# Three edits to an encoder layer: a second tile for v's parts with h written in pairs, w_out queued behind the first pages of y, and eight slices for the last h2

## The chip, the cores and the metric

The kernel runs on one core of one Trainium2 chip. The metric is device time in microseconds (us) for one execution of the whole layer, the median of the runs; the time before is 2748.61 us. A core has a matrix engine (TensorE, "PE" in the profile, with its weight loads as "PEld"), a vector engine (VectorE, "DVE"), an engine for activation functions (ScalarE, "ACT"), a general one (GpSimd, "POOL") and a sequencer that here only issues transfers (SyncE, "SP"). Each works through its own queue in order. ScalarE's queue also issues transfers (`A.dma_start`).

## The reference

One layer of an encoder with two kinds of attention side by side, 2048 tokens of width 1024, all in float32:

```
h  = RMSNorm(x)
z  = h @ W_in  -> [q_A | k_A | v_A | q_B | k_B | v_B | gate_A | gate_B]
yA = windowed GQA over |t-s| <= 128 with ALiBi and per-head sink logit
yB = 2-D neighbourhood attention on the (ROWS, GRID_W) token grid with a relative position bias
x  = x + ( sigmoid(gate_A) * (yA @ Wp_A) + sigmoid(gate_B) * (yB @ Wp_B) ) @ W_out
x  = x + relu(RMSNorm(x) @ W_up)^2 @ W_down
final RMSNorm
```

W_in is 1024 x 4352, Wp_A and Wp_B are 512 x 1024, W_out is 1024 x 1024, W_up is 1024 x 4096 and W_down 4096 x 1024.

## The kernel before

**Precision and products.** Every float32 operand of a large product is split into a high part (`hi`, a cast on ScalarE) and a low part (`lo`, a subtraction on VectorE or GpSimd), and each product is three matmuls (`mm3`, lines 193 to 195, or `mm3s`, lines 239 to 241): high by high, high by low, low by high. Tokens are worked on in four blocks of 512 (`b`, 0 to 3). Data on the chip lies transposed, features on the 128 partitions. The dense stage, the up projection and the down projection use a scheme of seven block products in place of eight (products 1 to 7, in the order 1, 2, 5, 6, 7, 4, 3 in the dense stage and 1, 5, 6, 2, 7, 4, 3 in the up projection). A group of columns that is put through the seven products is called a quad; in a quad each product has one or two column halves (`a`) of 12 matmuls.

**Order.** The code is not the order of execution. A planner, which works on its own estimate of times when the kernel is built, orders each engine's queue, with earlier code first when several things are ready, and adds the waits. A ring or pool with n buffers lets the (n+1)-th tile of that name be written only when the first has been read for the last time, by transfers too; memory of a closed pool goes to later pools, whose tiles wait for the old tiles on the same bytes. `tc.issue_after(i)` puts what is issued in its block on the engine of `i` behind `i` in that engine's queue; it does not wait for `i` to finish.

**Stages.**
- The dense stage computes z. Blocks 0 and 1 of x are normalised and transposed into pages of h that stay on the chip, and quads 0 to 8 of W_in's columns run over those two blocks: k and v of A, q of A, q of B, k of B, v of B (quad 4, `O_VB`), then four of the gates. Results go out to DRAM through SyncE. `in_e` ("ze" in the profile) is a ring of two tiles [128, 2, 512] used by results that are copied out of PSUM, by the squares of the normalisation (`Junk`) and by h of the blocks 2 and 3. A column tile of v goes through `v_parts` (line 334): four transposes, a cast of the high half on ScalarE (line 350) and a subtraction for the low half on VectorE (line 351) into the tile `in_v2` ("zv", one tile of [128, 1024]), and two writes on SyncE (line 402, `vs_b<-zv`). Quad 4 makes eight such tiles. Ahead of quads 4 and 5, blocks 2 and 3 of x are loaded (`x_tiles`, four tiles `xin`), normalised, transposed (line 229), scaled by ScalarE (line 448) into one half of a `ze` tile and written to `h1d` (line 566), eight slices of 256 KB per block.
- In the attention stages TensorE also computes z for the blocks 2 and 3 (from `h1d`, read back into tiles `hT`), with those products as filler between the attention's. The outputs go to DRAM as `y_a` and `y_b` on ScalarE's queue (`put` and `flush`, line 172).
- The merge, per block: `load_y` (line 889) loads the pages of y_a and y_b (`yraw`, line 897) and splits them (`page`, lines 903 and 904). For each of eight feature tiles `f`, weights of both projections are loaded and split (`whl`, line 175), products go to `mm` and `s` banks, gates (`z<-zg`) are applied, and `mh` and `ml` (one tile of [128, 8, 512] each) get the merged result. In block 0 each `f` is followed by `load_wo(f)` (line 921): a load of 512 KB of w_out into a tile `xr` on SyncE, a cast on ScalarE (line 925) and a subtraction on VectorE (line 926). Then come the output projection (`pt<-wo,mh`), the residual, the norm, and h2: for each of eight slices `k`, four transposes (line 1182) into a PSUM bank `av` or `pt`, a scaling on ScalarE (line 1184) into `h2s`, a ring of two tiles, and a write to `h2d` on ScalarE's queue.
- The up projection, whose first weights and right-hand pages (`ubh`, from lines 1033 on) are made before the merge ends, takes over the PSUM banks of the merge: its bank 5 is the first `pt` bank. The second half of product 6 uses that bank. Page 2 of the right-hand side (`bh2`, high and low) lies on the bytes of `mh`. Weights of products 1, 2 and 3 share one tile, `uwhla`.
- The down projection and the final norm follow.

Of the kernel before, what the change touches and what calls it, by code (L numbers as in the profile page):

```python
# [92 lines left out]
def encoder_layer(ctx, tc, x, norm_mix, w_in, b_gate, sink, rpb, w_pa, w_pb, w_out,  # L93
# [12 lines left out]
    def pools(stack, side, tags, name):  # L106

        return {t: pool(f"{name}_{t}", side=side, stack=stack) for t in tags}
# [118 lines left out]
    def turned(ps, tiles, k):  # L227
        for t in range(4):
            PE.transpose(ps[:, t * P : (t + 1) * P], tiles[t][:, k * P : (k + 1) * P], ident)
# [17 lines left out]
    def ring(stack, tag, shape, dt, bufs, side="right"):  # L247

        pl = pool(f"r_{tag}", side=side, stack=stack)
        return lambda: T(pl, shape, dt, tag, bufs)  # L250
# [17 lines left out]
    def zbank(pl, bufs=1):  # L268
        n_ps[0] += 1
        return pl.tile([P, 512], F32, tag="b", bufs=bufs, name=f"zb_{n_ps[0]}")  # L270
# [3 lines left out]
    s_x = ExitStack()  # L274
    xp = pools(s_x, "left", ("xin",), "x0")
    in_sum = ring(s_z, "zS", [P, 4, 256], F32, 2)
    in_v2 = ring(s_z, "zv2", [P, 1024], F32, 1)
    in_page[5] = ring(s_z, "zh5", PAGE, F32R, 2)
    in_c = ring(s_z, "zc", [P, BT], F32, 8)
    in_e = ring(s_z, "ze", [P, 2, BT], F32, 2)  # L280
# [53 lines left out]
    def v_parts(col, b, vt, p2, v2):  # L334

        for t in range(4):
            PE.transpose(p2[:, t * P : (t + 1) * P], vt[:, t * P : (t + 1) * P], ident)
        if col == O_VA:
            vv = v2.rearrange("p (e t z d) -> p e t z d", e=2, t=4, z=2)
            p2v = p2.rearrange("p (t e d) -> p e t d", t=4, e=2)  # L340
            dst = vs_a[b // 2].rearrange("e p c d -> p e (c d)")[:, :, b % 2 * BT : (b % 2 + 1) * BT]
            out = [(dst, v2.rearrange("p (e d) -> p e d", e=2))]
        else:
            vv = v2.rearrange("p (r e c z d) -> p r e c z d", r=2, e=2, c=2, z=2)
            p2v = p2.rearrange("p (c r e d) -> p r e c d", c=2, r=2, e=2)
            dst = vs_b[(col - O_VB) // P].rearrange("(x r s) b f -> x r s b f", r=2, s=2)
            out = [(dst[:, :, i, b], v2[i * GW : (i + 1) * GW].rearrange("p (r f) -> p r f", r=2)) for i in range(2)]
        z = 3 if col == O_VA else 4
        hi, lo = (vv[(slice(None),) * z + (n,)] for n in range(2))
        A.copy(hi.bitcast(F32R), p2v)  # L350
        V.tensor_tensor(out=lo.bitcast(F32R), in0=p2v, in1=hi, op=ALU.subtract)
        return out
# [37 lines left out]
    def in_result(col, b, src, in_psum):  # L390

        if col < O_VB and col != O_VA:
            for dst, t in qk_parts(col, b, src, in_e()):
                SY.dma_start(dst, t)
            return
        if in_psum:
            t = in_e()[:, 0]
            A.copy(t, src)
            src = t
        if is_v(col):  # L400
            for dst, t in v_parts(col, b, src, zbank(tpool, 2), in_v2()):
                SY.dma_start(dst, t)
        else:
            f = (col - O_GA) // P
            SY.dma_start(zg[b][0][f // 8, (f % 8) * P : (f % 8 + 1) * P, :], src)
# [41 lines left out]
    def scaled(out, ps, k):  # L447
        A.activation(out, ps, AF.Copy, scale=g_mix[:, k : k + 1])
# [82 lines left out]
        next(quad0)  # L531
        next(quad1)
    s_kv.close()
    xp = pools(s_z, "right", ("xin", "st"), "x2")
    ws = in_weights(*QUADS[2])

    def bias_tables():
# [10 lines left out]
            SY.dma_start(tabs[n], tb)  # L548

    for q in range(2, len(QUADS)):  # L550
        if q == 7:
            bias_tables()
        lf = list(in_left(ws, 256))
        if q + 1 < len(QUADS):
            ws = in_weights(*QUADS[q + 1])
        if q in (4, 5):

            b = q - 2
            xt = x_tiles(xp, b, 4)
            normalised(xp, xt, Junk())  # L560
            for k in range(KC):
                ps = zbank(tpool, 2)
                turned(ps, xt, k)
                ht = in_e()[:, 0]
                scaled(ht, ps, k)
                SY.dma_start(h1d[b - 2][k * P : (k + 1) * P, :], ht)
        for _ in in_quad(*QUADS[q], iter(lf), right):
            pass
    s_z.close()
# [141 lines left out]
    def paced(filler, pieces, total, lag):  # L711

        for n in pieces:
            at = n * 32 // total - lag
            with tc.issue_after(done[at]) if at >= 0 else nullcontext():
                next(filler, None)
# [172 lines left out]
    def load_y(b):  # L889
        yh, yl = [], []  # L890
        for n in range(2):
            h = T(p4, [P, 4, BT], F32R, "page", 4)
            l = T(p4, [P, 4, BT], F32R, "page", 4)
            for c in range(4):
                raw = T(p4, [P, BT], F32, "yraw", 6)
                src = (y_a[c // 2][(c % 2) * P : (c % 2 + 1) * P] if n == 0 else y_b[c])[:, b * BT : (b + 1) * BT]
                SY.dma_start(raw, src)
                hc, lc = h[:, c], l[:, c]
                if n == 1:

                    raw = flipped(raw)
                    hc, lc = (t.rearrange("p (r j c) -> p j r c", r=8, j=4) for t in (hc, lc))
                A.copy(hc, raw)
                V.tensor_tensor(out=lc, in0=raw, in1=hc.bitcast(F32), op=ALU.subtract)
            yh.append(h)
            yl.append(l)
        return yh, yl

    first_y = load_y(0)
    paced(fill, range(20, 44), 40, 4)  # L910
    s_h.close()

# [8 lines left out]
    def load_wo(n):  # L921
        rv = T(p4x, [P, D], F32, "xr", 4)
        SY.dma_start(rv, w_out[0][n * P : (n + 1) * P, :])
        hl = T(pwo, [P, 2, D], F32R, "wo", 8)
        A.copy(hl[:, 0], rv)
        V.tensor_tensor(out=hl[:, 1], in0=rv, in1=hl[:, 0].bitcast(F32), op=ALU.subtract)
        wo.append(hl)
# [209 lines left out]

    for b in range(NB):
        yh, yl = first_y if b == 0 else load_y(b)
        mh = T(p4x, [P, KC, BT], F32R, "mh", 1)  # L1140
        ml = T(p4x, [P, KC, BT], F32R, "ml", 1)
        for f in range(8):
            hl = slice_of([(cols(w_pa[0], f * P), 4), (cols(w_pb[0], f * P), 4)])
            parts = []
            for n in range(2):
                ps = psum("mm" if n == 0 else "s", 2 if n == 0 else 3)
                for c in range(4):
                    mm3(ps, hl[:, 0, 4 * n + c, :], hl[:, 1, 4 * n + c, :], yh[n][:, c], yl[n][:, c], c == 0, c == 3)
                g = T(wp, [P, 2, BT], F32, "z", 2)[:, 0] if n else T(p4, [P, BT], F32, "z", 4)
                SY.dma_start(g, zg[b][0][n, f * P : (f + 1) * P, :])  # L1150
                A.activation(g, g, AF.Sigmoid, bias=bg[:, 8 * n + f : 8 * n + f + 1])
                V.tensor_tensor(out=g, in0=ps, in1=g, op=ALU.mult)
                parts.append(g)
            G.tensor_tensor(out=parts[0], in0=parts[0], in1=parts[1], op=ALU.add)
            A.copy(mh[:, f], parts[0])
            V.tensor_tensor(out=ml[:, f], in0=parts[0], in1=mh[:, f].bitcast(F32), op=ALU.subtract)
            if b == 0:
                load_wo(f)
        if b == NB - 1:
            s_pg.close()  # L1160
            s_w.close()
            up_start()
        tiles = []
        for t in range(4):
            row0 = b * BT + t * P
            xt = load_tile(p4x, "xr", 4, xf[row0 : row0 + P])
            for c in range(2):
                xc = xt[:, c * BT : (c + 1) * BT]
                ps = psum("pt", 2)
                for k in range(KC):  # L1170
                    mm3(ps, mh[:, k, t * P : (t + 1) * P], ml[:, k, t * P : (t + 1) * P],
                        wo[k][:, 0, c * BT : (c + 1) * BT], wo[k][:, 1, c * BT : (c + 1) * BT], k == 0, k == KC - 1)
                V.tensor_tensor(out=xc, in0=ps, in1=xc, op=ALU.add)
            flush()
            put(x2d[b][t * P : (t + 1) * P], xt)
            tiles.append(xt)
        flush()
        normalised(p4x, tiles)
        for k in range(KC):
            ps = psum("av", 1) if b < NB - 1 or k % 3 == 0 else psum("pt", 2)  # L1180
            for t in range(4):
                PE.transpose(ps[:, t * P : (t + 1) * P], tiles[t][:, k * P : (k + 1) * P], ident)
            ht = T(ph2, [P, BT], F32, "h2s", 2)
            A.activation(ht, ps, AF.Copy, scale=g_mlp[:, k : k + 1])  # L1184
            put(h2d[b][k * P : (k + 1) * P, :], ht)
            flush(1)
# [211 lines left out]
```

## Time and profile before

| | |
|---|---|
| median of 3 runs | 2748.61 us (2748.01 to 2757.35) |
| the profiled execution | 2750.41 us, its span 2748.6 us |
| mean granted TensorE clock | 0.986 |
| busy TensorE / VectorE / ScalarE / GpSimd | 2658.3 / 1551.9 / 1250.2 / 839.6 us |
| HBM read and written | 323.28 MB and 155.26 MB, 174 GB/s over the span |

The span is the time from the first to the last instruction in the profile. "Busy" counts the time in which an engine works on an instruction; waiting and issuing transfers are not counted. The chain that ended last is followed back from the end of the execution: each step names what the next one waited for. In a timeline, a row is start, length, engine, line, operation, tile written and tiles read, shape and count; in brackets stands the idle time of the engine just before it and what ended that.

### The profile page before, as it was taken

What the parts mean: (1) busy time and instruction counts of PE and PEld (TensorE: products, weight loads), DVE (VectorE), ACT (ScalarE), POOL (GpSimd) and SP (SyncE); (2) the same over time, 40 slices, a digit from 0 to 9 for tenths busy, and PEclk for the clock granted to TensorE, in tenths of its full rate; (3) what the DMA queues carried; (4) which work ended last, traced back from release to release, by engine and by line L of the source; (5) the groups of instructions that cost most, each with busy time, mean ns of one, the idle gap of its engine ahead of it and who ended that gap; (6) DMA issues with size and microseconds to landing.
All of it is one profiled execution on the core that took longest, in us unless ns stands there. A gap on an engine that the chain in (4) does not pass through costs nothing.

```text
span 2748.6 us, 35115 instructions
## 1 busy us (share of the span) xinstructions
PE 2658.3 (97%) x12332; PEld 2190.2 (80%) x12332; DVE 1551.9 (56%) x2352; ACT 1250.2 (45%) x2225; POOL 839.6 (31%) x671
## 2 busy tenths in 40 slices
PE   7998998999999999899999899989999999999998
PEld 6886877777788888787887788878888888888887
DVE  8754447676454444543435567586654644546667
ACT  6343236665455555534533444554444332322444
POOL 1111223334455552433420365555544000000000
PEclk9999999999999999999999999999999999999999
DMA  4855274446677665746534656574444954445555
GB/s 148 229 152 176 98 228 141 114 115 175 179 208 199 179 172 148 234 145 197 187 107 181 224 175 201 185 228 146 143 141 161 338 179 154 145 156 173 179 183 175
DMA packets 329664, 480.86 MB, mean 175 GB/s; under 512 B 28024, under 2 KB 162296, under 8 KB 327312
## 3 DMA queue, kind: packets, MB, share of 16 engines
q1 hardware_dynamic: 300560, 445.06, 51.5%
q10 hardware_dynamic: 28928, 33.56, 3.8%
q8 instruction: 97, 1.59, 0.2%
q14 instruction: 79, 0.65, 0.1%
HBM read 323.28 MB, written 155.26 MB: 174 GB/s over the span
## 4 chain that ended last, share of the span: by engine, by line
PE 85%; DMA 6%; DVE 5%; ACT 2%; issue 1%; POOL 0%; SPq 0%; ACTq 0%; POOLq 0%; DVEq 0%
PE b L239 14%; PE b L241 14%; PE b L240 14%; PE mm L193 5%; PE mm L195 5%; PE mm L194 5%; PE zb L241 3%; PE zb L240 3%; PE zb L239 3%; PE pt L193 2%; PE pt L195 2%; PE pt L194 2%; PE av L848 2%; PE pt L837 2%; PE s L810 2%
## 5 line engine op out<-in xcount | busy, mean ns | idle before, releaser
L240 PE MATMUL b<-dwh,dah 128*128 128x512 f32 x896 | 348.5, 389 | 0.0
L241 PE MATMUL b<-dwh,dah 128*128 128x512 f32 x896 | 347.7, 389 | 0.0
L239 PE MATMUL b<-dwh,dah 128*128 128x512 f32 x896 | 338.1, 389 | 1.5 <-ACT dwh L235 1.5
L232 POOL TENSOR_TENSOR uc<-uc,uc 128x512 f32<-128x512 f32 x120 | 233.3, 1958 | 206.8 <-issue 150.1
L235 ACT CAST dah<-da 128x1024 fp32r<-128x1024 f32 (+1 forms) x128 | 121.0, 945 | 366.4 <-PE b L241 243.1
L236 DVE TENSOR_TENSOR dah<-da,dah 128x1024 fp32r<-128x1024 f32 (+1 forms) x128 | 139.3, 1089 | 221.4 <-ACT dah L235 218.3
L239 PE MATMUL b<-ubh,uwhlb 128*128 128x512 f32 x592 | 232.2, 392 | 6.2 <-ACT h2s L1184 5.4
L241 PE MATMUL b<-ubh,uwhlb 128*128 128x512 f32 x592 | 231.3, 392 | 2.6 <-DVE uwhlb L236 2.6
L240 PE MATMUL b<-ubh,uwhlb 128*128 128x512 f32 x592 | 232.0, 392 | 0.0
L193 PE MATMUL mm<-hT,whl 128*128 128x512 f32 x544 | 220.7, 406 | 4.7 <-ACT whl L175 2.4
L232 DVE TENSOR_TENSOR uc<-b,uc 128x512 f32<-128x512 f32 x160 | 109.1, 688 | 203.1 <-PE b L241 162.6
L195 PE MATMUL mm<-hT,whl 128*128 128x512 f32 x544 | 217.0, 399 | 1.2 <-POOL whl L176 1.2
L194 PE MATMUL mm<-hT,whl 128*128 128x512 f32 x544 | 216.1, 397 | 0.0
L176 POOL TENSOR_TENSOR whl<-raw,whl 128x1024 fp32r<-128x1024 f32 x66 | 159.4, 2416 | 159.2 <-ACT whl L175 138.1
L1288 POOL TENSOR_TENSOR st<-st,power 128x1 f32<-128x1 f32 x16 | 13.6, 857 | 613.6 <-DVE st L1287 613.5
L239 PEld LDWEIGHTS b<-dwh,dah 128*128 128x128 f32 x896 | 168.1, 188 | 36.7 <-ACT dwh L235 1.9
L240 PEld LDWEIGHTS b<-dwh,dah 128*128 128x128 f32 x896 | 168.2, 188 | 34.9
L241 PEld LDWEIGHTS b<-dwh,dah 128*128 128x128 f32 x896 | 168.2, 188 | 34.8
L239 PE MATMUL zb<-zh,zwhl 128*128 128x512 f32 x476 | 190.4, 402 | 3.8 <-DVE zh L451 2.6
L240 PE MATMUL zb<-zh,zwhl 128*128 128x512 f32 x476 | 189.9, 400 | 1.8 <-DVE zh L236 1.8
L241 PE MATMUL zb<-zh,zwhl 128*128 128x512 f32 x476 | 187.5, 399 | 0.6 <-DVE zwhl L236 0.5
L239 PEld LDWEIGHTS b<-ubh,uwhlb 128*128 128x128 f32 x592 | 112.1, 189 | 30.2 <-ACT h2s L1184 5.7
(241 smaller groups left out, 6235.4 us busy)
## 6 DMA issues: line engine op xcount, KB each, us to landing
at<-uc SPq DMA_DIRECT2D x224, 256.0 KB
da<-at SPq DMA_DIRECT2D x96, 512.0 KB
dw<-in_w_down_dram SPq DMA_DIRECT2D x160, 256.0 KB
uraw<-in_w_up_dram SPq DMA_DIRECT2D x32, 1024.0 KB
raw<-in_w_in_dram SPq DMA_DIRECT2D x34, 512.0 KB
zraw<-in_w_in_dram SPq DMA_DIRECT2D x16, 1024.0 KB
z<-zg SPq DMA_DIRECT2D x64, 256.0 KB
xin<-in_x_dram SPq DMA_DIRECT2D x16, 512.0 KB
```

What stands on the lines that cost most here:

```text
L176: G.tensor_tensor(out=hl[:, 1], in0=raw, in1=hl[:, 0].bitcast(F32), op=ALU.subtract)
L193: PE.matmul(ps, lh, rh, start=first, stop=False)
L194: PE.matmul(ps, lh, rl, start=False, stop=False)
L195: PE.matmul(ps, ll, rh, start=False, stop=last)
L232: return eng.tensor_tensor(out=out, in0=a, in1=b, op=op).ins
L235: A.copy(hi, src)
L236: eng.tensor_tensor(out=lo, in0=src, in1=hi.bitcast(F32), op=ALU.subtract)
L239: PE.matmul(ps, lh, rh, start=first, stop=False, skip_group_check=True)
L240: PE.matmul(ps, lh, rl, start=False, stop=False, skip_group_check=True)
L241: PE.matmul(ps, ll, rh, start=False, stop=last, skip_group_check=True)
L810: PE.matmul(ps[:, :n], q[:, i, :], kv[:, z, B_R0[i] // 4 : (B_R0[i] + B_NR[i]) // 4, 4 * B_C0[j] : 4 * (B_C0[j] + w)], start=z == 0, stop= ...
L837: PE.transpose(pt[:kp, at + (i - i0) * P : at + (i - i0 + 1) * P], s[i][:, rr : rr + kp], ident)
```

## The change

There are three edits.

1. In the dense stage, v's parts of quad 4 use a new ring `zv3` of two tiles, in a pool that is open from after quad 1 until quad 5 (the old single tile serves quad 0). The pool for `xin` opens in its place at quad 5, so the blocks 2 and 3 of x are handled ahead of quads 5 and 6 and no longer ahead of 4 and 5. Two slices of h now share one `ze` tile, and each pair is one write of 512 KB.
2. The loads of w_out are queued behind the last load of the first pages of y on SyncE. The casts are not ordered by hand.
3. For the last block, h2 is written into one tile of eight slices in the place of `mh`, in place of the two tiles `h2s`.

```diff
-    in_v2 = ring(s_z, "zv2", [P, 1024], F32, 1)
+    in_v2 = [ring(s_z, "zv2", [P, 1024], F32, 1)]
...
-            for dst, t in v_parts(col, b, src, zbank(tpool, 2), in_v2()):
+            for dst, t in v_parts(col, b, src, zbank(tpool, 2), in_v2[-1]()):
...
     s_kv.close()
-    xp = pools(s_z, "right", ("xin", "st"), "x2")
+    s_v = ExitStack()
+    in_v2.append(ring(s_v, "zv3", [P, 1024], F32, 2))
     ws = in_weights(*QUADS[2])
...
     for q in range(2, len(QUADS)):
+        if q == 5:
+            s_v.close()
+            in_v2.pop()
+            xp = pools(s_z, "right", ("xin", "st"), "x2")
         if q == 7:
             bias_tables()
...
-        if q in (4, 5):
-
-            b = q - 2
+        if q in (5, 6):
+
+            b = q - 3
             xt = x_tiles(xp, b, 4)
             normalised(xp, xt, Junk())
-            for k in range(KC):
-                ps = zbank(tpool, 2)
-                turned(ps, xt, k)
-                ht = in_e()[:, 0]
-                scaled(ht, ps, k)
-                SY.dma_start(h1d[b - 2][k * P : (k + 1) * P, :], ht)
+            for k in range(0, KC, 2):
+                ht = in_e()
+                for i in range(2):
+                    ps = zbank(tpool, 2)
+                    turned(ps, xt, k + i)
+                    scaled(ht[:, i], ps, k + i)
+                SY.dma_start(h1d[b - 2][k * P : (k + 2) * P, :].rearrange("(k p) t -> p k t", p=P), ht)
...
-                SY.dma_start(raw, src)
+                last_dma[0] = SY.dma_start(raw, src).ins
...
     first_y = load_y(0)
+    first_load = last_dma[0]
...
             if b == 0:
-                load_wo(f)
+                with tc.issue_after(first_load):
+                    load_wo(f)
...
-            ht = T(ph2, [P, BT], F32, "h2s", 2)
+            if b == NB - 1:
+                h2 = T(p4x, [P, KC, BT], F32R, "mh", 1).bitcast(F32) if k == 0 else h2
+                ht = h2[:, k]
+            else:
+                ht = T(ph2, [P, BT], F32, "h2s", 2)
```

## The prediction

> **What bounds the kernel now.** I read the page first, then the chain that ended last in order of time, then the timelines of the engines around the breaks in that chain, and last a table of windows for those breaks.
>
> ```profile
> span 2748.6 us, 35115 instructions
> ...
> PE 2658.3 (97%) x12332; PEld 2190.2 (80%) x12332; DVE 1551.9 (56%) x2352; ACT 1250.2 (45%) x2225; POOL 839.6 (31%) x671
> ...
> PE 85%; DMA 6%; DVE 5%; ACT 2%; issue 1%; POOL 0%; SPq 0%; ACTq 0%; POOLq 0%; DVEq 0%
> ```
>
> TensorE is busy 2658.3 of 2748.6 us. The change alters no matrix product and no transpose, so all that it can win directly is idle time of TensorE (90 us in all) and the time at half clock that follows an idle stretch. It touches three places. The windows show each with the stretch behind it (columns: length; busy time of PE, PEld, DVE, ACT and POOL with counts; granted clock; share of the DMA engines; GB/s).
>
> ```profile
> 130.00:200.00 70.00, 70.00 (x316) 56.99 (x315) 42.82 (x51) 32.23 (x47) 13.56 (x8) 1.00 0.57 151
> ...
> 212.00:266.00 54.00, 45.59 (x219) 36.51 (x219) 26.38 (x37) 20.71 (x39) 8.48 (x6) 1.00 0.57 165
> ...
> 265.70:269.10 3.40, 3.40 (x12) 2.67 (x13) 2.49 (x3) 2.19 (x3) 0.00 (x0) 0.50 0.67 249
> 1115.30:1123.60 8.30, 0.06 (x1) 0.00 (x0) 4.89 (x5) 4.70 (x5) 0.00 (x0) 0.72 1.04 362
> 1123.60:1129.30 5.70, 5.19 (x11) 3.17 (x12) 3.79 (x6) 3.99 (x5) 1.87 (x1) 0.50 1.00 358
> 1519.00:1527.10 8.10, 1.03 (x8) 0.56 (x6) 7.15 (x5) 4.53 (x6) 1.34 (x1) 0.67 0.41 155
> 1527.10:1532.10 5.00, 4.98 (x12) 3.80 (x12) 0.00 (x0) 0.00 (x0) 0.00 (x0) 0.51 0.95 285
> ```
>
> Place 1, the dense stage with v's columns: 54.00 - 45.59 = 8.4 us idle, then 3.4 us at clock 0.50, which loses 1.7: 10.1 us. Place 2, the start of the merge: 8.3 us idle, then 5.19 us of work at half clock, 2.6 lost: 10.9 us. Place 3, the last h2: 8.10 - 1.03 = 7.1 us idle, then 2.5 lost: 9.6 us. Together they hold 30.6 us.
>
> **Part 1, v's parts and h.** ScalarE's timeline, with the idle time before each cast of a part of v in quad 4, and TensorE's three stalls there:
>
> ```profile
> 226.66 0.59 ACT L350 CAST zv<-zb 128x512 fp32r<-128x512 f32 x1 [4.49 <-DMA vs_b<-zv]
> ...
> 258.10 0.58 ACT L350 CAST zv<-zb 128x512 fp32r<-128x512 f32 x1 [5.67 <-DMA vs_b<-zv]
> ```
>
> ```profile
> 246.06 0.63 PE L337 MATMUL zb<-ident,zc 128*128 128x128 f32 x4 [2.38 <-DVE zv L351]
> ...
> 259.56 1.06 PE L229 MATMUL zb<-ident,xin 128*128 128x128 f32 x8 [1.93 <-DVE zv L351]
> ...
> 265.63 1.10 PE L229 MATMUL zb<-ident,xin 128*128 128x128 f32 x4 [3.62 <-ACT ze L448]
> ```
>
> With one tile, each part waits for the write of the one before. The third cast starts at 226.66 and the eighth at 258.10, so a round takes 31.4 / 5 = 6.3 us, and eight take 50. TensorE's products of a quad are 7 x 2 x 12 = 168, at 70.00 / 316 = 0.22 us some 37 us, so v's chain is the longer one and TensorE stalls on it (2.38 and 1.93). With two tiles the chain is 25 us and lies beside the products. That removes both.
>
> The third stall is h's: eight slices of x block 3 pass through the two `ze` tiles, each held by a write to h1d.
>
> ```profile
> 1.64 6.32 DMA xin<-in_x_dram
> ...
> 206.29 5.58 DMA h1d<-ze
> ...
> 260.69 4.09 DMA h1d<-ze
> ...
> 371.31 0.95 ACT hT L235
> ```
>
> A write of 256 KB takes 4.1 to 5.6 us; with two tiles, eight slices are four rounds of about 5.5 us with their casts, 22 us. In pairs there are two rounds. A pair's write of 512 KB does not occur; the nearest transfer of that size is the load at 6.32, so a round is about 7.7 us, 15 us in all. Every other instruction of the two blocks moves by one quad: eight loads, 16 squares, the scalings, 64 transposes. On SyncE the loads now stand behind v's writes, and two of the four `xin` tiles lie on the bytes of the new v tiles, so their loads wait until v's last writes have landed; queued behind them on SyncE are the gate columns' writes and the next weights, which have a quad (37 us) to spare. A load of 6.32 and about 6 us of squares and scaling then lie beside quad 5's products. What hides this is the product stream: block 2's slices lie in 130 to 212, where TensorE is 70.00 of 70.00 us busy. If the cover is missing, a block costs what block 3 costs now, 3.6 idle plus 1.7 of half clock, so the unknown is 0 to 5.3 per block. I take 1 for each, near the block that cost nothing. h1d's readers start at 371.31, some 50 us after the later quad. Part 1 wins 10.1 - 2 = 8 us.
>
> **Part 2, w_out.** SyncE's, ScalarE's and TensorE's timelines, and from the chain two writes and a load for size:
>
> ```profile
> 1110.00 1.82 SPq L923 DMA_DIRECT2D xr<-in_w_out_dram  x4
> ...
> 1119.40 0.34 SPq L897 DMA_DIRECT2D yraw<-y_b  x1
> ```
>
> ```profile
> 1112.48 0.53 ACTq L172 DMA_DIRECT2D y_b<-yb  x1
> ...
> 1122.04 1.04 ACT L925 CAST wo<-xr 128x1024 fp32r<-128x1024 f32 x1 [2.21 <-DMA xr<-in_w_out_dram]
> 1122.99 0.61 ACT L903 CAST page<-yraw 128x512 fp32r<-128x512 f32 x1
> ```
>
> ```profile
> 1123.65 0.79 PE L193 MATMUL s<-page,whl 128*128 128x512 f32 x1 [8.29 <-ACT page L903]
> ```
>
> ```profile
> 635.51 4.01 DMA y_a<-ya
> ...
> 709.35 2.58 DMA y_a<-ya
> ...
> 1223.75 2.73 DMA z<-zg
> ```
>
> The last page of y needs the last output of the attention. Its write of 128 KB goes out at 1113.0 and the load behind it at 1119.40: 6.4 us, where writes of that size took 2.58 and 4.01. In between the DMA engines are full (share 1.04): four loads of w_out, 2 MB, were issued just before. Then ScalarE waits for a fifth load of w_out ahead of the page's cast. With w_out behind the first pages, the write lands at 1115.6 to 1117.0; 0.34 for the issue, 2.73 for a load of 256 KB and 0.61 for the cast let TensorE go on at 1119.3 to 1120.7 and not at 1123.65. That is 2.9 to 4.4 us, I take 3.6. The shorter stall leaves less half clock; I take the same share of the 2.6, 0.9. The eight casts (1.04 each on ScalarE, and as many subtractions on VectorE) leave the stall and go beside the first tiles of the merge; queued behind them on ScalarE are the casts of the projections' weights, which TensorE needs. One such wait was 2.21, so this is 0 to 4.4 us if two are exposed; I take 0.5, since after 1123.65 three of these casts stood there already and TensorE lost only 5.70 - 5.19 = 0.5. Part 2 wins 4 us.
>
> By the Trainium skill, "DMA: Bandwidth & Descriptors", section on queues, rings and completion order, each DMA engine goes round-robin between the queues that have work. By that, ScalarE's write would not stand behind SyncE's loads, w_out would not be what delays it, and part 2 would win about 0.5 and not 4. The 6.4 against 2.58 to 4.01 speaks against it. By "TensorE: Matmul & The Clock Gate", Part 1, one full idle window of about 3.4 us halves the clock and one busy window restores it, so no stall would cost over 1.7 behind it; the trace has 2.6 at place 2.
>
> **Part 3, the last h2.** ScalarE's timeline, TensorE's, and two writes from the chain:
>
> ```profile
> 1504.26 2.01 ACT L235 CAST ubh<-urb 128x1024 fp32r<-128x1024 f32 x2
> ...
> 1514.72 0.69 ACT L1184 ACTIVATE h2s<-pt,g_mlp 128x512 f32<-128x512 f32 x1 [2.16 <-DMA h2d<-h2s]
> ...
> 1526.38 0.69 ACT L1184 ACTIVATE h2s<-pt,g_mlp 128x512 f32<-128x512 f32 x1 [1.50 <-DMA h2d<-h2s]
> ```
>
> ```profile
> 1508.89 0.62 PE L239 MATMUL b<-ubh,uwhla 128*128 128x512 f32 x2
> ...
> 1527.12 0.80 PE L239 MATMUL b<-ubh,uwhlb 128*128 128x512 f32 x1 [5.44 <-ACT h2s L1184]
> ...
> 1533.18 0.50 PE L239 MATMUL b<-ubh,uwhlb 128*128 128x512 f32 x1 [0.78 <-DVE uc L232]
> ```
>
> ```profile
> 1515.44 4.76 DMA h2d<-h2s
> ...
> 1524.33 2.03 DMA h2d<-h2s
> ```
>
> With two `h2s` tiles, ScalarE waits for the writes, and the second half of product 6 waits for the bank that the last slice frees at 1527.1. With eight slices ScalarE needs 8 x 0.69 = 5.5 us from about 1509.7, some 1516 with the issues.
>
> The edit also adds a wait. h2 takes `mh`'s tile, and the two pages of `bh2` lie on exactly those bytes (90080 to 106464 of each partition). Now their casts run at 1504.26 and product 2 (`uwhla`, from 1508.89) fills TensorE while h2 is written. After, the casts wait until the last write of h2 has landed. Behind them on ScalarE stand the casts of page 4, which is made from the same block, and of later weights; product 3's weights need the tile that product 2 reads. The last write goes out at 1516 and takes 2.0 to 4.8 us: 1518 to 1521, and with a half cast (1.0) and its subtraction product 2 starts at 1520.5 to 1523. Until then TensorE has product 7 and the second half of 6, 36 x 0.22 = 8 us, and the last transposes, about 2.5: from 1508.9 to about 1519.5. So it idles 1 to 3.5 us, and has done products 2, 6 and 7 by 1526 to 1528.5. Now it has that when the half of product 7 that starts at 1533.18 ends, 1535.9. The gain is 7.4 to 9.9 us; page 4, later by the same wait, may take 1.4 to 3.9 of it. Part 3 wins 6 us.
>
> **Sum.** 8 + 4 + 6 = 18 us. The profiled execution took 2750.41 us (span 2748.6 and 1.8 around it), 1.8 over the median of the runs, 2748.61. From the median: 2730.6 us.
>
> **Rivals.**
> (a) Slower. Place 3: the eight writes of h2 go one after the other on ScalarE's queue at the 5.58 us of a loaded write, 45 us from 1510. Product 2 then starts at 1557 and runs at half clock (10.6) to 1568, against 1535.9 now: 32 lost, 12 won elsewhere, 2768.6 us. It decides from a last landing at about 1525 for the place and 1537 for the whole. For it: bh2's bytes are h2's. Against it: the write that began at 1524.33 took 2.03, so writes overlap.
> (b) Place 1 wins nothing: the planner that orders TensorE puts block 2's transposes ahead of tiles that now wait for v's last writes, and quads 5 and 6 stall for 10 us as quad 4 does now: 18 - 8 = 10 won, 2738.6 us. For it: `xin` on v's bytes. Against it: a whole quad of cover.
> (c) The write of y is not late because of w_out, the round-robin case: 14.5 won, 2734.1 us. For it: the write goes out on ScalarE's own queue. Against it: the same write was two to four us faster with free engines.
> (d) Two parts fail, or the planner, which orders the whole program anew, loses elsewhere what is won: about 2743 us.
>
> **How the numbers follow.** Forecast 0.53; (a) 0.07; (b) 0.20; (c) 0.10; (d) 0.10. A measurement here tells about 0.5% (13.7 us) from no change. The forecast is beyond that, half of (c) too: faster 0.58. (b), (d) and the other half of (c) lie within: 0.35. (a) is slower: 0.07. The range goes from nearly all of the 30.6 us won (2719) to just past (d) (2746), which leaves out (a) and the edges.
>
> **What would show it.** Right: no ScalarE wait for `vs_b<-zv` over 1 us in quad 4; the stall ahead of the first `s<-page` product near 4 us; eight h2 activations within 7 us; a wait of a `ubh` cast for a write of h2, with TensorE idle under 4 us there. Wrong: TensorE waiting for `xin` or `ze` in quads 5 or 6 for over 4 us; the write of y_b still taking over 6 us; product 2 of the first up quad starting after 1525.

## The result, and the profile after

The changed kernel takes 2742.72 us (median of 18 runs, 2734.92 to 2751.37), the kernel before 2751.46 us (18 runs, 2747.73 to 2758.06). The ratio is 0.9967, 95% interval 0.9957 to 0.9976: 9 us faster, half of the 18 us that were forecast. Two more comparisons of the same order of instructions gave 0.9962 and 0.9948 (below). The profiled execution took 2739.11 us. From its page, the span and the busy times:

```profile
span 2737.3 us, 35101 instructions
...
PE 2654.3 (97%) x12332; PEld 2185.1 (80%) x12332; DVE 1558.6 (57%) x2352; ACT 1248.0 (46%) x2225; POOL 843.0 (31%) x671
```

TensorE's busy time fell by 4 us (the work done at half clock cost 28.0 us before and 24.0 after) and its idle time by 7 (90.3 to 83.1).

**Place 1.** ScalarE's timeline of quad 4 (two of the casts of v's parts), the window of the whole dense stage after its start, and from the page the writes of h in pairs (KB each, median us from issue to landing):

```profile
207.48 0.59 ACT L350 CAST zv<-zb 128x512 fp32r<-128x512 f32 x1
...
218.59 0.59 ACT L350 CAST zv<-zb 128x512 fp32r<-128x512 f32 x1
```

```profile
60.00:376.90 316.90, 316.26 (x1420) 256.59 (x1418) 184.52 (x213) 120.55 (x169) 51.99 (x32) 1.00 0.59 173
```

```profile
h1d<-ze SPq DMA_DIRECT2D x8, 512.0 KB, 5.0
```

No cast waits for a write of v any more. TensorE works 316.26 of 316.90 us at full clock: place 1 is gone, quads 5 and 6 with the moved blocks of x included. A pair's write takes 5.0 us.

**Place 2.** ScalarE's, SyncE's and TensorE's timelines at the start of the merge, and the window behind the stall (the columns are those of the prediction's windows):

```profile
1105.54 0.53 ACTq L172 DMA_DIRECT2D y_b<-yb  x1
1112.03 0.62 ACT L909 CAST page<-yraw 128x512 fp32r<-128x512 f32 x1 [6.15 <-DMA yraw<-y_b]
```

```profile
1108.17 0.34 SPq L903 DMA_DIRECT2D yraw<-y_b  x1
1108.57 2.12 SPq L930 DMA_DIRECT2D xr<-in_w_out_dram  x4
```

```profile
1112.70 1.22 PE L193 MATMUL s<-page,whl 128*128 128x512 f32 x2 [4.43 <-ACT page L909]
```

```profile
1112.70:1118.40 5.70, 5.07 (x14) 3.12 (x14) 3.65 (x5) 4.57 (x6) 2.82 (x2) 0.71 1.03 405
```

The write of y goes out at 1106.07 and its load at 1108.17: 2.1 us where it took 6.4. The eight profiles in which w_out is loaded as before show 6.1 to 7.5 us there, the twelve with edit 2 show 2.0 to 2.4. The stall is 4.43 and not 8.29, and in this profile the clock behind it is 0.71 and not 0.50.

**Place 3.** ScalarE's timeline, first and last of the eight scalings of h2 and the casts behind them, and TensorE's:

```profile
1503.05 0.69 ACT L1196 ACTIVATE mh<-av,g_mlp 128x512 f32<-128x512 f32 x1 [4.02 <-PE av L1190]
...
1508.37 0.69 ACT L1196 ACTIVATE mh<-pt,g_mlp 128x512 f32<-128x512 f32 x1 [0.19 <-ACT mh L1196]
...
1513.47 1.05 ACT L235 CAST uwhlb<-uraw 128x1024 fp32r<-128x1024 f32 x1 [2.54 <-PE b L241]
1514.42 2.00 ACT L235 CAST ubh<-urb 128x1024 fp32r<-128x1024 f32 x2
```

```profile
1499.09 0.50 PE L239 MATMUL b<-ubh,uwhlb 128*128 128x512 f32 x1 [1.30 <-ACT uwhlb L235]
...
1509.11 0.79 PE L239 MATMUL b<-ubh,uwhlb 128*128 128x512 f32 x1 [2.34 <-ACT mh L1196]
...
1517.21 0.61 PE L239 MATMUL b<-ubh,uwhla 128*128 128x512 f32 x2
```

The eight scalings take 6.0 us (1503.05 to 1509.06). In this profile the casts of page 2 (1514.42) wait for no write; ahead of them a cast of weights waited for TensorE. TensorE still has stalls of 1.30 and 2.34 us.

**The end of the merge**, some 60 us earlier, was not in the forecast. First the kernel before, TensorE and VectorE, then the changed kernel, TensorE, ScalarE and VectorE:

```profile
1457.88 0.80 PE L193 MATMUL pt<-wo,mh 128*128 128x512 f32 x1 [3.90 <-DVE xr L1173]
```

```profile
1454.78 2.35 DVE L232 TENSOR_TENSOR uraw<-uraw,uraw 128x1024 f32<-128x1024 f32 x2
1457.14 1.29 DVE L1173 TENSOR_TENSOR xr<-pt,xr 128x512 f32<-128x512 f32 x2
1458.34 2.35 DVE L236 TENSOR_TENSOR ubh<-uraw,ubh 128x1024 fp32r<-128x1024 f32 x2
```

```profile
1447.47 0.80 PE L239 MATMUL b<-ubh,uwhla 128*128 128x512 f32 x1 [5.86 <-ACT uwhla L235]
```

```profile
1443.40 0.69 ACT L1196 ACTIVATE h2s<-av,g_mlp 128x512 f32<-128x512 f32 x1 [2.50 <-DMA h2d<-h2s]
...
1446.38 1.04 ACT L235 CAST uwhla<-uraw 128x1024 fp32r<-128x1024 f32 x1
```

```profile
1445.56 2.36 DVE L236 TENSOR_TENSOR ubh<-uraw,ubh 128x1024 fp32r<-128x1024 f32 x2 [2.46 <-ACT ubh L235]
1447.84 1.22 DVE L236 TENSOR_TENSOR uwhla<-uraw,uwhla 128x1024 fp32r<-128x1024 f32 x1
...
1451.37 1.28 DVE L1181 TENSOR_TENSOR xr<-pt,xr 128x512 f32<-128x512 f32 x2
```

The planner made another order. Before, VectorE's addition that empties the `pt` banks (`xr<-pt,xr`) stands ahead of the second subtraction for page 1. Now it stands behind that, the weights' subtraction and two more, at 1451.37; and product 1 of the up projection (`b<-ubh,uwhla`) has been put into the hole. Its weights come no sooner than 1447.4, behind a scaling of block 2 that waits for a write. SyncE's order differs as well: the first weights of the up projection are loaded at 1433.29, 8 us ahead of the block of x for the addition (`xr`, 1441.31); in the kernel before they go out behind it (1455.52 and 1453.69). All kernels below with edit 2, up to the last two, have the first of these orders, all without it the second.

From the traces, idle time of TensorE plus the time lost at half clock (busy time at clock 0.5, halved), in us, means where there is more than one profile. The numbers at the top are the edits that a kernel holds, X is an exchange of two pages and D puts an addition first on VectorE, both below. The last row is the elapsed time from the start of the stall at place 2 to the start of the stall of 4.5 us ahead of the second half of the up projection (before: 1115.36 to 1802.76). It also holds the middle of the merge, which no other row has and which loses 3.4 us in the kernel before and 0.6 to 3.9 in the others.

| | none | 1 | 2 | 3 | 1+3 | 1+2+3 | 1+2+3+X | 1+2+3+D | 1+2+3+X+D |
|---|---|---|---|---|---|---|---|---|---|
| profiles | 1 | 1 | 1 | 1 | 2 | 3 | 3 | 1 | 1 |
| dense stage after 60 us | 10.5 | 0.9 | 12.7 | 11.3 | 0.5 | 1.0 | 0.8 | 0.4 | 0.6 |
| attention | 37.5 | 40.4 | 38.2 | 39.2 | 40.6 | 39.2 | 41.7 | 46.0 | 39.0 |
| start of the merge | 11.3 | 11.4 | 7.5 | 11.9 | 11.5 | 7.5 | 7.9 | 7.4 | 7.9 |
| end of the merge | 6.8 | 7.0 | 9.2 | 6.8 | 6.9 | 9.1 | 8.9 | 7.4 | 8.3 |
| last h2 and behind it | 10.3 | 10.3 | 12.5 | 6.0 | 5.2 | 8.3 | 4.7 | 5.2 | 2.1 |
| elapsed | 687.4 | 684.7 | 688.1 | 683.9 | 679.8 | 684.2 | 679.2 | 678.1 | 675.3 |

The single 687.4 is not exact as a starting point: edit 1 changes no code of that stretch, and the kernel with edit 1 alone has 684.7, the two kernels below with a part of edit 1 have 688.0 and 685.2.

### The profile page after: what moved, and what is told of

The parts are those of the page before. It is cut to its first block, busy times and chain, and to the rows that moved or that the text cites. A ratio compares the mean times of both kernels' runs of the same rounds, so it can differ in the third digit from the quotient of the medians.

```text
span 2737.3 us, 35101 instructions
## 1 busy us (share of the span) xinstructions
PE 2654.3 (97%) x12332; PEld 2185.1 (80%) x12332; DVE 1558.6 (57%) x2352; ACT 1248.0 (46%) x2225; POOL 843.0 (31%) x671
```

## The experiments

**One edit at a time.** Each kernel is the kernel before with the lines of one edit of the change's diff; in the fourth the whole change has page 2 on other bytes:

```diff
-    up_homes("bh6", "bh2", "bh3", "chunk", "rb", "c", "bh7", "bh4")
+    up_homes("bh6", "bh4", "bh3", "chunk", "rb", "c", "bh7", "bh2")
```

> The first edit alone (two tiles for v's parts, x blocks 2 and 3 one quad later, h in pairs); the merge and the last h2 as before. Theory A (the parts add; what the profile of the full change lost again at the start of the attention and of the down projection is chance of the run): TensorE's idle time in the dense stage falls by 8 to 10 us, nothing is added elsewhere, the time is 9 to 10 us under the one before. Theory B (the new order makes the planner lay out the attention worse): the dense stage wins the same 8 to 10 us, but the first 100 us of the attention stage show 2 to 4 us more idle time than before, as they do with the full change, and the time is only 5 to 7 us lower.

> The second edit alone (w_out queued behind the first pages of y). Theory A: the write of the last y_b lands about 4 us sooner, the idle time ahead of the first s<-page product falls from 8.3 to about 4.4 us as with the full change, the time is 4 us lower, and nothing else moves. The round-robin rival: the write takes as long as before, the stall stays above 7 us, and the time is within 1 us of before.

> The third edit alone (eight slices for the last h2 in mh's place). Theory A (ScalarE no longer waits, but product 2 of the first up quad, which waits for the tile's last write, is missing as filler): idle time around the last h2 falls by about 2 us of the 7.9, the time is 2 to 4 us lower. Rival (the slices win all that was forecast, and what was lost in the full change came from the other edits): 6 us lower. Rival (the stall at the start of up product 1, 5.9 us with the full change against 3.9 before, comes from this edit): the time is 0 to 1 us lower.

> All three edits, with the places of the pages bh2 and bh4 exchanged, so that h2 lies on the bytes of page 4 and page 2 lies where w_out was. Theory A (what is left at the last h2 is product 2 missing as filler): product 2 runs while h2 is written, the 2.3 us stall at the second half of product 6 and the smaller ones go, page 4 may wait 0 to 2 us, and the time is 2 to 4 us under that of the full change, 11 to 13 under the one before. Rival (the bank of the last slice sets it): as the full change, within 1 us.

Edit 1 alone: 2740.74 us, ratio 0.9951 (0.9939 to 0.9963). Edit 2 alone: 2753.50, 1.0005 (0.9996 to 1.0013). Edit 3 alone: 2748.58, 0.9983 (0.9974 to 0.9992). The exchange: 2735.05, 0.9935 (0.9923 to 0.9947). Edit 1 won more than theory A's 9 to 10 us. Edit 3 won 4 to 5 us, theory A's 2 to 4 or a little more. The exchange came out 9 us under the changed kernel by the ratios, more than theory A's 2 to 4; later runs show less. Edit 2 took its 4 us at the start of the merge (11.3 to 7.5 in the table), as its theory A had it, and still moved the time by nothing. Its profile has the other order at the end of the merge too:

```profile
1457.92 0.79 PE L239 MATMUL b<-ubh,uwhla 128*128 128x512 f32 x1 [5.51 <-ACT uwhla L235]
```

**Without edit 2, and the halves of edit 1.** The changed kernel again; edits 1 and 3; the same with the exchange; and edit 1 with h stored slice by slice as before:

```diff
-            for k in range(0, KC, 2):
-                ht = in_e()
...
+            for k in range(KC):
+                ps = zbank(tpool, 2)
+                turned(ps, xt, k)
+                ht = in_e()[:, 0]
```

> The changed kernel once more, for a second profile and for a comparison with the next kernels on one chip. Theory A (the 8.7 us of the median are what the three edits bring here, and the differences between profiled runs at the start, such as a gap of 2.43 us at 19.66, come and go): ratio 0.996 to 0.9975 again, some 8 us; the end of the merge again shows a stall of 5 to 6 us ahead of the first product of the up-projection (b<-ubh,uwhla), since the planned order is the same; the start of the attention shows other gaps of 1 to 3 us. Theory B (the first comparison was a poor draw): ratio 0.9935 or below, 18 us as the version with exchanged homes showed.

> Edits 1 and 3, w_out loaded as before. Theory A (edit 2 wins 4 us at the start of the merge and the order of the up-projection's first product gives it back at the end of the merge): no stall over 5 us ahead of b<-ubh,uwhla near 1440, but one near 4.4 ahead of pt<-wo; the start of the merge stalls 8 to 9 us; the time is that of the changed kernel within 3 us, some 2741. Theory B (edit 2 keeps its 4 us when it stands with the others): 4 us slower than the changed kernel, 2746. Theory C (edit 2 costs when it stands with the others, as edit 1 alone at -13.5 against -8.7 for all suggests): 5 us faster than the changed kernel, 2737 or below.

> Edits 1 and 3 with bh2 and bh4 exchanged in the list of homes, w_out loaded as before. Against the changed kernel with the same exchange (2735.05): theory A gives the same within 3 us; theory B gives 2739; theory C gives 2730. At the last h2 all gaps together should be 3 to 4 us and not 6, because product 2 no longer waits for the bytes of h2 and is there to fill the time.

> Edit 1 without the pairs: two tiles for v's parts, the two x blocks one quad later, h stored one slice at a time as before. Theory D (v's one tile and the quad in which the blocks stand made the stalls of the dense stage): as edit 1 alone, 2741, no wait for ze over 1 us. Theory E (the pairs do half of it): TensorE stalls on ze about 3.6 us for a block, each with 1.7 of half clock behind it, in quads 5 and 6: 2746 to 2751.

The changed kernel: 2740.31, 0.9962 (0.9951 to 0.9974). Edits 1 and 3: 2735.50, 0.9945 (0.9933 to 0.9958); with the exchange 2737.98, 0.9948 (0.9933 to 0.9962), no gain from the exchange there. Theory B (edit 2 keeps its gain in company) fell. Theory C fits, 5 us, though the intervals overlap; in the stretch that it is about, the elapsed times are 678.9 and 680.6 us without edit 2 and 681.7 to 685.8 with it. Without pairs: 2747.31, 0.9983 (0.9973 to 0.9993), 3.7 us left in the dense stage, mostly here (TensorE):

```profile
263.23 0.50 PE L239 MATMUL zb<-zh,zwhl 128*128 128x512 f32 x1 [2.15 <-ACT ze L398]
```

Both theories on the pairs were partly right: in the dense stage two tiles and the later quads take 6.7 of the 10.5 us and the pairs the rest, and the stalls of 3.6 us that theory E expected are not there; the time is where theory E put it.

**A hold on product 1.** The first two products of the up projection are queued on TensorE behind the output projection of rows `t` of the last block, t = 0 at first:

```diff
+            if t == 0:
+                held[0] = last_mm
...
+                    with tc.issue_after(held[0]) if (m, q) == (0, 0) and n in (1, 5) else nullcontext():
```

With it ran the same with the exchange, the exchange once more, and the pairs alone (the kernel before with h written in pairs, for `q in (4, 5)`).

> The changed kernel, with the first two products of the up-projection queued on TensorE behind the output projection's products of the first 128 rows of x block 3 (order alone, no wait). Theory A (edit 2's 4 us are given back because the new order puts product 1 at 1441, where its weights are not cast yet, so that it fills nothing and is missing at the last h2): the stall of 5.9 us ahead of b<-ubh,uwhla is gone, one of about 4.1 ahead of pt<-wo stands there, idle and half clock at the end of the merge fall from 8.2-9.4 to about 6.7 and at the last h2 from 7.5-10.3 to about 6; some 4 us faster than the changed kernel, ratio to before about 0.9945. Theory B (the time lost lies elsewhere, in the eight casts of w_out that moved, or in chance): the same time as the changed kernel, 0.9962 to 0.9967.

> The same order, with bh2 and bh4 exchanged in the list of homes as well. Theory A: 2 to 4 us faster than the exchange alone, ratio about 0.992, and the lowest of all versions, 2731 to 2733. Theory B: as the exchange alone, 0.9935.

> The exchange of bh2 and bh4 alone once more, beside the two kernels above. If product 2 free of h2's bytes is worth what the last h2's gaps say (6.9 to 10.3 us of idle and half clock against 5.6), ratio 0.9935 to 0.995, 3 to 7 us faster than the changed kernel. If its first 0.9935 was a good draw: 0.996.

> h stored in pairs and nothing else: one tile for v's parts, the two x blocks in their old quads. Theory D (v's one tile makes most of the dense stage's 10 us): TensorE still waits 2.4 and 1.9 us for DVE zv in quad 4, the wait for ze (3.6) is gone, 3 to 5 us won, 2747 to 2749. Theory E (the slow store of h is what holds everything up): no stall is left and the gain is that of all of edit 1, 2741.

The products of t = 0 stand ahead of the stall anyway, so the order was that of the changed kernel and neither theory was tested; the run is a third comparison of it: 2738.77, 0.9948 (0.9936 to 0.9960). With the exchange 2738.43, 0.9944 (0.9932 to 0.9956); the exchange alone 2737.40, 0.9945 (0.9933 to 0.9956). Pairs alone: 2747.84, 0.9980 (0.9970 to 0.9991), 6.2 us left in the dense stage. The wait for `ze`, which both theories had gone, is 2.55 us where it was 3.62. ScalarE still waits for v's writes in that kernel, TensorE less than before (2.38):

```profile
236.71 0.59 ACT L350 CAST zv<-zb 128x512 fp32r<-128x512 f32 x1 [4.41 <-DMA vs_b<-zv]
```

```profile
238.07 0.66 PE L337 MATMUL zb<-ident,zc 128*128 128x128 f32 x4 [1.10 <-DVE zv L351]
```

The hold was then tried with `t == 1`, in the changed kernel, with the exchange, and with edit 2 alone; edits 1 and 3 ran beside them.

> The changed kernel with the first two products of the up-projection queued on TensorE behind the output projection of the second 128 rows of x block 3 (the first try named the first 128 rows, which stand ahead of the stall anyway, so that its order was that of the changed kernel). Theory A (edit 2's win is given back because product 1 stands on TensorE's queue before its weights are cast, fills nothing there and is missing at the last h2): the stall of 5.9 us ahead of b<-ubh,uwhla is gone and one of about 4.1 ahead of pt<-wo stands there; idle and half clock from the start of the merge to the start of the second half of the up-projection come down by 2 to 5 us; the time is 2 to 5 us under the changed kernel's, ratio to before 0.993 to 0.995. Theory B (chance, or the casts of w_out): no difference to the changed kernel's three comparisons, 0.9948 to 0.9967.

> The same hold with bh2 and bh4 exchanged. Theory A: 2 to 4 us under the exchange alone (0.9935, 0.9945, and 0.9944 for the first try of the hold): 0.992 to 0.9935. Theory B: 0.994.

> Edit 2 (w_out) alone with the hold. Edit 2 alone had won 4 us at the start of the merge and the whole time had not moved (1.0005). Theory A: with the old order at the end of the merge the win stays: ratio 0.9975 to 0.999, idle and half clock of some 6.8 at the end of the merge and 10.3 at the last h2 as in the kernel before, where edit 2 alone had 9.2 and 12.5. Theory B: 1.0005 again.

> Edits 1 and 3 once more, for the comparison with the first kernel of this call, which is the same and edit 2 with the hold. Theory A: the held kernel is 2 to 5 us faster than this one, because the 4 us at the start of the merge are then won and kept. Theory B: this one is as fast or faster, ratio 0.9945 again.

The changed kernel with the hold: 2741.39, 0.9965 (0.9952 to 0.9977); with the exchange 2736.45, 0.9946 (0.9934 to 0.9959); edit 2 alone with the hold 2750.78, 0.9992 (0.9983 to 1.0001), between its two theories; edits 1 and 3 again 2735.52, 0.9944 (0.9931 to 0.9957). Theory A fell: the product went out of the way and the stall got longer. TensorE and VectorE in the first:

```profile
1454.44 0.80 PE L193 MATMUL pt<-wo,mh 128*128 128x512 f32 x1 [10.64 <-DVE xr L1182]
```

```profile
1450.17 1.22 DVE L236 TENSOR_TENSOR uwhla<-uraw,uwhla 128x1024 fp32r<-128x1024 f32 x1
1451.31 1.22 DVE L232 TENSOR_TENSOR uS<-uraw,uraw 128x1024 f32<-128x1024 f32 x1
1452.56 1.22 DVE L232 TENSOR_TENSOR uraw<-uraw 128x1024 f32<-128x1024 f32 x1
1453.70 1.28 DVE L1182 TENSOR_TENSOR xr<-pt,xr 128x512 f32<-128x512 f32 x2
```

The addition stands in line behind subtractions that wait for ScalarE's casts. Its own data were there some 6 us earlier, by an estimate from the run below, where the load of `xr` lands 4 us behind the last transposes. Product 1 in the hole was a patch on the stall and not its cause. What the hold gained at the last h2 (8.3 to 4.6), it lost here.

**The addition first.** The preparations of the up projection are queued on VectorE behind the addition, in the changed kernel and in the one with the exchange. Their code also moves behind the first 128 rows of block 3, so that the planner may order the other engines anew too; SyncE has `xr` ahead of the weights again, as without edit 2, so these runs do not separate VectorE's order from that.

```diff
-            up_start()
...
+                freed = V.tensor_tensor(out=xc, in0=ps, in1=xc, op=ALU.add).ins
+            if b == NB - 1 and t == 0:
+                with tc.issue_after(freed):
+                    up_start()
```

> The changed kernel with the first preparations of the up-projection (up_start) queued on VectorE behind the addition that empties TensorE's bank after the first 128 rows of x block 3; in all kernels with edit 2 that addition stood behind four preparations, one of which waits for ScalarE and, through it, for a write of block 2's h2. Theory A2 (VectorE's order is what gives edit 2's 4 us back, and product 1 only filled part of the hole): TensorE's stall at the end of the merge falls from 5.9 (10.6 with the product held) to 1 to 4 us; from the start of the merge to the second half of the up-projection the span falls from 681.7-685.8 to 675-680; the ratio to before is 0.993 to 0.995, 3 to 5 us under the changed kernel. Theory B2 (the stall has yet another cause behind VectorE's order, such as the load of xr): the stall stays at 4 us or more, now released by the load, and the time is the changed kernel's, 0.996.

> The same with bh2 and bh4 exchanged in the list of homes: the best that the runs point to. Theory A2: 3 to 5 us under the exchange alone (0.9935 to 0.9946), 0.9915 to 0.993, with the last h2 at 4 to 5.6 us of idle and half clock. Theory B2: as the exchange alone.

2737.11 us, 0.9941 (0.9927 to 0.9954), and 2730.19 us, 0.9918 (0.9905 to 0.9932): the fastest version, 8 to 13 us under the changed kernel by the ratios and 5 to 8 under the exchange alone. The stall did not fall to 1 to 4 us, as theory A2 had it; TensorE, VectorE and ScalarE in the first of the two:

```profile
1449.83 0.79 PE L193 MATMUL pt<-wo,mh 128*128 128x512 f32 x1 [4.77 <-DVE xr L1180]
```

```profile
1449.09 1.29 DVE L1180 TENSOR_TENSOR xr<-pt,xr 128x512 f32<-128x512 f32 x2 [8.90 <-DMA xr<-in_x_dram]
```

```profile
1513.64 2.00 ACT L235 CAST ubh<-urb 128x1024 fp32r<-128x1024 f32 x2 [0.57 <-DMA h2d<-mh]
```

Now the load of `xr` is what comes last, as theory B2 said, and so it is in the second run of edits 1 and 3, without edit 2 (VectorE):

```profile
1444.94 1.29 DVE L1179 TENSOR_TENSOR xr<-pt,xr 128x512 f32<-128x512 f32 x2 [0.32 <-DMA xr<-in_x_dram]
```

But the elapsed time of the stretch is 678.1 us, in the 675 to 680 of A2 and 6 under the changed kernel; with the exchange it is 675.3 and not 679.2. The stall is about as long as without edit 2 (3.9 to 4.5), and product 1 is no longer spent on it, so that more products are left to fill the time of the last h2 (8.3 to 5.2 us). The cast in the last ScalarE line, of page 2, waits for a write of h2.

## Why the prediction was half right

**Part 1, forecast 8, was right.** The dense stage went from 10.5 to 1.0 us in its three profiles. A pair's write took 5.0 us where 6.32 was taken, and the unknown of 0 to 5.3 per block came out near 0; rival (b) fell. The attention shows 37.1 to 46.5 us of idle and half clock in the profiles with the moved quads, 37.5 to 41.3 in the others: some of the win may be given back there, in waits that differ from run to run; that stays open. That edit 1 alone won 13.5 us by its ratio (interval 10 to 17; 11.6 by the medians), more than the 9.6 of its dense stage, is not explained.

**Part 2, forecast 4, was right in its place and wrong in the sum.** The stall (4.43 us, forecast 3.9 to 5.3), the write's 2.1 us and the 3.8 us in the table bear it out; rival (c) fell. (The "same share" of the 2.6 us at half clock, 3.6 of 8.29, is 1.1 and not the 0.9 of the prediction; that changes little.) By the Trainium skill, "DMA: Bandwidth & Descriptors", section on queues, rings and completion order, a DMA engine goes round-robin between the queues that have work; the write on ScalarE's queue took 6.4 us with SyncE's four loads ahead of it and 2.1 without, so here that turn-taking did not keep it from being held up. The step that failed is "Part 2 wins 4 us" as a term of its own: it costed the casts that leave the stall, and not that the planner orders all that follows anew. With edit 2 the planner put product 1 and the preparations of the up projection ahead of the addition that empties the bank. In the three profiles that cost 2.3 us at the end of the merge (6.8 to 9.1), and at the last h2, where the 24 matmuls of product 1 were already used up, 3.1 us more than in edits 1 and 3 (8.3 against 5.2): together 5.4 us, more than the 3.8 won. In time edit 2 won nothing alone (1.0005), and edits 1 and 3 without it are 1 to 6 us faster than the whole change; with the exchange they are not (0.9948 against 0.9935 to 0.9945).

**Part 3, forecast 6, was too large, and in company more so.** In its place it won 4.4 us alone, 5.1 with edit 1 and 2.0 in the whole change. The eight scalings took 6.0 us (forecast under 7). The wait for h2's writes exists but is small: no cast of page 2 shows it in the first profile, and it is 0.57 to 0.90 us in three kernels in which product 1 comes later (addition first, hold, edits 1 and 3 again). Product 2 was to start 10.8 to 13.3 us after the first scaling (1509.7 to 1520.5 and 1523); it started 14.2 us after it (1503.05 to 1517.21), and 14 to 17 in the other profiles of the whole change, behind casts of weights that come earlier in ScalarE's queue and wait for TensorE or, in the second profile, for 2.80 us that are put down to a write of h2. So the term that was too small is the idle time left at the last h2, 1 to 3.5 us in the forecast; there is 5.7 to 6.9, small gaps included, in the three profiles, besides what half clock costs. What sharing h2's bytes costs is that product 2 cannot fill the time in which h2 is made: the exchange brought the last h2 from 8.3 to 4.7 us. Rival (a) fell: product 2 started at 1517.21 and not at 1557.

**The sum.** Parts 2 and 3 together were to win 10 us. Of the 28.4 us that the start and the end of the merge and the last h2 lose in the kernel before, the whole change wins 3.5, edits 1 and 3 win 4.8, and the whole change with the addition first wins 8.4. The elapsed row has 3.2, 7.6 and 9.3, with up to 2.8 us of it from the middle of the merge; one order differs there by up to 4 us between profiles. By the ratios the addition first is worth 2 to 7 us (0.9941 against 0.9948 to 0.9967), and 5 to 8 with the exchange (0.9918 against 0.9935 to 0.9945). So most of what was missing lay in the new order at the end of the merge, which the trace shows on VectorE. Rival (d) named it ("loses elsewhere what is won", 2743 us) with a chance of 0.10 only; it named no place, so that its number came out is in part luck. Why the planner turned that order round can't be seen in a trace, and edit 2 alone with the addition first was not run. Of the 12 us between 2730.6 and 2742.72, another 3 are the starting point: 2748.61 was the median of three runs, and eighteen gave 2751.46.

**The half clock.** Forecast 0.9 less behind the shorter stall. In the clock records the stretch at half clock around place 2 is 10.24 us in the kernel before and 3.41 in the changed one, with 6.83 in its second profile. By "TensorE: Matmul & The Clock Gate" of the Trainium skill the gate watches a free-running window of about 3.4 us; nearly all stretches in these records are 3.4, 6.8 or 10.2 us long, which agrees, and within each of the 20 profiles they all start a whole number of steps of 3.413 us apart. The bound of 1.7 us behind a stall, which the prediction worked out from one such window and saw broken by the 2.6 at place 2, was too low: the window in which the stall ends can stay at half clock as well as the next one, and 2.8 us were lost in that second profile. Nor does it take a full idle window here: in the kernel before a stall of 1.76 us that ends at 43.46 is followed by half clock from 43.83 to 47.24.

## What to carry to other kernels

When a planner orders the queues, a transfer moved at one place is a change to the order of everything behind it: look, in the trace of the change, for the in-order queue on which a short instruction that frees a bank has come to stand behind one that waits. A product that fills a stall may be a patch on it: moving the filler showed the real releaser, and with that one instruction ordered first the win stayed. When a buffer shares bytes with another, ask not only when its reader may start but which stall that reader was filling.

## What the runs showed of the hardware that was not expected

A write of 128 KB on one engine's queue took three times as long (6.4 against 2.1 us; 6.1 to 7.5 against 2.0 to 2.4 over all profiles) when 2 MB of loads had been issued on another engine's queue just before. And two profiles of one and the same order differ by 3.5 us in the elapsed row (681.7 and 685.2), with gaps such as one of 2.4 us at 19.7 us that are there in one execution (13 of the 20) and not in the next: single profiles tell where the time is, but parts of 4 us need several of them.
